# K-to-gate handover, blocked k, shared value buffers and branch A's split order in a one-core transformer block

## The chip, the cores and the metric

The kernel runs on one core of one Trainium2 chip. The metric is the device time of one execution in microseconds, the median over several runs. A profiled execution has a span, from its first to its last instruction, and a time of its own that is a little longer.

## The reference

One layer of a hybrid block over 1024 tokens of width 1024, in float32:

```python
h = rmsnorm(x, ln1_g[l]) * (1.0 + sc1) + sh1
p = h @ w_in[l]
q, k, v, cb, cc, cx, ga, gb = jnp.split(p, split_at, axis=-1)      # eight sections of 1024
q = rmsnorm(q.reshape(b, s_len, SB_HEADS, SB_HEAD_DIM), q_norm_g[l])   # 16 heads of 64
k = rmsnorm(k.reshape(b, s_len, SB_HEADS, SB_HEAD_DIM), k_norm_g[l])
...
y_a = stick_breaking_attention(q, k, v)
y_b = cb * causal_dwconv(cc * cx, conv_w[l])
merged = (jax.nn.sigmoid(ga) * (y_a @ w_branch_a[l])
          + jax.nn.sigmoid(gb) * (y_b @ w_branch_b[l]))
x = x + g1 * (merged @ w_out[l])
h = rmsnorm(x, ln2_g[l]) * (1.0 + sc2) + sh2
f = (jax.nn.silu(h @ w_ffn_gate[l]) * (h @ w_ffn_up[l])) @ w_ffn_down[l]
x = x + g2 * f
```

The modulations sh, sc and g come from a small product of the conditioning vector with `ada_w`.

## The kernel before

Every float32 product is computed from operands that are each split into a high part (ScalarE, a rounding copy) and a low part (VectorE, the difference), with three matmuls: high by high, high by low, low by high. Activations live on chip in four large tiles of 128 x 8 x 512: `hh[n]` is the high part and `hl[n]` the low part of the normalised input for token half n. Weights are loaded by SP's DMA queue into a small pool `raw` and split into the pools `whi` and `wlo`.

The program is one long sequence of stages, written in program order. A planner (a list scheduler that simulates times) fixes the order of instructions on each engine; each engine then runs strictly in that order and waits on semaphores. `tc.high_priority()` moves instructions ahead in the planner's order; `tc.issue_after(ins)` puts instructions of one engine behind `ins` on that engine. In some stretches `in_order` pins the order as written.

The stages are:

1. The start: the norm, the modulations, the splits of the input, half of v.
2. K (the loop over `cc` and `i`): for each half `cc` of the key width and each tile `i` of 128 tokens, `mm_tok` makes 24 matmuls into one PSUM bank. `finish_k` squares it (into a tile of the `wlo` pool, four slots), normalises it per head, transposes it on TensorE, splits it into `khl` and stores high and low part to DRAM (`d_k`) by ScalarE's DMA queue. The second halves of `finish_k` run one or two tokens later as `tails`. Beside K the generator `factors` prepares Strassen factors of the input in DRAM (`d_t`), which SP loads later.
3. The gates: 20 pairs of weight blocks (`gates`: q, the two convolution sections, the two gate sections), each computed with seven products in place of eight (Strassen's scheme in Winograd's form). Gate g needs two raw weights of 128 x 1024, the four quarters a11, a12 and a21, a22. GpSimd forms s3 = a11 − a21, s2 = a22 − s3, s1 = a21 + a22 and s4 = a12 − s2. The products are p1 (a11), p2 (a12), p6 (s2), p5 (s1), p7 (s3), p3 (s4) and p4 (a22), by the factors `fac[0]` to `fac[6]`. `first_two` makes p1 and p2 of gates 0 and 1 ahead of the stage, from raws that are loaded for that alone; gate 0 and gate 1 then load their two raws again. `fac[3]` lies over the first half of `hh[1]` and `hl[1]`, so it can be loaded only when K has read these. `fac[6]` (2 MB) and all of the stage's tiles lie in the pool `gp`, over the memory of K's weights and tiles. VectorE adds the products up; beside the last gates the later modulations are summed (`mods_later`, loads by ScalarE's queue). TensorE has six PSUM banks `pj` here.
4. The entry of attention: the second half of v is computed by `fillers`, first half e = 0 and then e = 1, each in eight blocks `i` of 24 matmuls of 256 columns. ScalarE evicts each block to a 256-wide tile `vs` (line 926) in the buffers of `ybh` and `ybl`, two of each, and SP stores it to `d_v`. The first half runs ahead of attention, beside the loads of heads 0 and 1 (`att_load`, with 64 partitions a load). Two PSUM banks `pj` serve here.
5. Attention over 16 heads, its TensorE order written out by hand, with the convolution branch and branch B's product as fillers between its steps.
6. Branch A: the attention output is read back from `d_ya` (`yr`), split into `ya` (line 1058 and the VectorE line behind it), and multiplied by `w_a` in 16 blocks; each is gated by sigmoid tiles and added to branch B's part. `preload_wo` loads five of the out projection's eight weight splits ahead (lines 1039 to 1044), through one raw slot.
7. The out projection, the second norm, the feed-forward part with Strassen again, and the output.

Line 132 to 134 are the three matmuls of a Strassen product, line 137 is the helper for two-operand element work on any engine, lines 309, 922 to 924 and 903 to 905 are the matmuls of K, of the value half and of the branches. Line 490 is the high half of `g_split`, line 412 the high half of k, line 479 a raw load, line 643 the load of `fac[6]`, line 554 the modulation sum, line 927 the store of a value block, line 1043 the high half of an out weight, line 1074 the gating of a block of branch A, line 1227 the first matmul of the out projection.

Of the kernel before, what the change touches and what calls it, by code (L numbers as in the profile page):

```python
# [30 lines left out]
def block_kernel(tc, x, x_t, cols, ada_1, ada_2, ada_row, w_q, w_kv, w_v1, w_cg, w_a, w_b, w_o, w_g, w_u, w_d, out):  # L31
# [36 lines left out]
    d_k = [drp.tile([KT, P, T], F32, name=f"d_k{e}") for e in range(2)]  # L68
# [327 lines left out]
    def finish_k(ps, i, ch):  # L396
# [54 lines left out]
    for cc in (1, 2):  # L451
        w = wq[4:] if cc == 1 else [load_w(w_kv[cc, j]) for j in range(4)]
        for i in range(8):
            ps = ps_pj()
            mm_tok(ps, i, w, 0, 8)
            while len(tails) >= 2:
                next(tails.pop(0), None)
            tails.append(finish_k(ps, i, cc - 1))
            next(tails[-1])
            for _ in range(2 if (cc, i) < (1, 4) else 3):  # L460
                more()
            if (cc, i) == (2, 1):
                for _ in ml:
                    pass
                s2b.close()
                sx.close()

    ftx = ExitStack()
    ftp = ftx.enter_context(tc.tile_pool(name="phft", bufs=1, side="right", reuse_waits="tile"))
    ft = {q: ftp.tile([P, 2, 4, 512], F32R, name=f"ft{q}") for q in (5, 4)}  # L470
    for q in (5, 4):
        nc.sync.dma_start(ft[q].bitcast(F32), d_t[q])

    def g_bank():
        return ps_pj()

# [16 lines left out]

    fac = {0: (hh[0][:, 0:4], hl[0][:, 0:4]), 1: (hh[0][:, 4:8], hl[0][:, 4:8]), 2: (hh[1][:, 4:8], hl[1][:, 4:8])}
    def g_prod(w, q):
# [4 lines left out]
    gates = ([(5, j) for j in range(4)] + [(sec, j) for j in range(4) for sec in (1, 2)] +  # L500
             [(sec, j) for sec in (4, 3) for j in range(4)])

    def w_of(sec, m):
        return w_q[m] if sec == 5 else w_cg[sec, m]

    pre = {}

    def first_two(g):
        sec, j = gates[g]
        raw = g_raw(w_of(sec, j))  # L510
        return g_prod(g_split(raw[:, :512]), 0), g_prod(g_split(raw[:, 512:]), 1)
# [7 lines left out]
    def two_raw(g):  # L519
        sec, j = gates[g]  # L520
        return g_raw(w_of(sec, j)), g_raw(w_of(sec, j + 4))
# [119 lines left out]
    raws = two_raw(0)  # L641
    pend, pmm, eq = [], [], end_q()
    nc.sync.dma_start(ft[6].bitcast(F32), d_t[6])
    for e in range(2):
        nc.sync.dma_start(fac[3][e].bitcast(F32), d_t[3][:, e])
    for g, (sec, j) in enumerate(gates):
# [38 lines left out]
        p6 = g_prod(g_split(s2_), 5)  # L685
# [934 lines left out]
```

## Time and profile before

| | |
|---|---|
| median of 3 runs | 1833.43 us (1831.43 to 1839.17) |
| profiled execution, own time | 1836.9 us |
| its span | 1835.0 us |
| TensorE busy | 1802.3 us (98%) |
| VectorE busy | 1353.1 us (74%) |
| ScalarE busy | 794.9 us (43%) |
| GpSimd busy | 366.7 us (20%) |
| mean granted TensorE clock | 0.996 |

A matmul of 512 columns shows as 0.39 us but the next one starts some 0.23 us later: they are pipelined, so the step between starts is the rate, and the time in brackets on a timeline row is real idle time. The granted clock is 1 nearly throughout; a window of few microseconds shows where it is not.

### The profile page before, as it was taken

The page shows a single profiled execution, that of the slowest core. Times are in us where ns is not written, and L with a number is a line of the kernel's source. Part 1 is how long each engine was busy: PE and PEld are TensorE (multiplying, and loading weights), DVE is VectorE, ACT ScalarE, POOL GpSimd, SP SyncE. Part 2 cuts the span into 40 slices and gives each one's busy share as a digit, 9 for nine tenths or more (in the row PEclk, how much of TensorE's full clock was granted, in tenths as well). Part 3 has the DMA queues.
Part 4 walks back from the last instruction along what each step waited for, and adds up shares of the span by engine and source line. Part 5 has one row for each costly group of instructions (what it writes and reads, how often), then busy time and mean ns, then how long its engine had stood idle before and what let it go on. Part 6 is the DMA issues. An engine that isn't in the chain of part 4 may idle for free.

```text
span 1835.0 us, 24920 instructions
## 1 busy us (share of the span) xinstructions
PE 1802.3 (98%) x8829; PEld 1503.8 (82%) x8829; DVE 1353.1 (74%) x1957; ACT 794.9 (43%) x1494; POOL 366.7 (20%) x277
## 2 busy tenths in 40 slices
PE   7999999999999999999999999999999999999999
PEld 4787778888878988888888788877888888888887
DVE  7874776779872789999888545589977788744776
ACT  3452553333332666666665311663444344422321
POOL 0043327423240000000000000105544454300000
PEclk9999999999999999999999999999999999999999
DMA  9598452227747467669654536424533344299766
GB/s 395 200 315 303 162 187 79 81 75 253 269 153 234 138 187 202 195 201 304 170 155 146 196 124 219 135 98 153 203 138 148 130 171 172 103 335 342 282 229 222
DMA packets 147268, 358.03 MB, mean 195 GB/s; under 512 B 15480, under 2 KB 44480, under 8 KB 144968
## 3 DMA queue, kind: packets, MB, share of 16 engines
q1 hardware_dynamic: 101816, 289.12, 46.6%
q10 hardware_dynamic: 44320, 63.64, 9.9%
q0 software_dynamic: 1008, 3.67, 0.5%
q8 instruction: 71, 1.16, 0.3%
q14 instruction: 53, 0.43, 0.1%
HBM read 245.74 MB, written 110.66 MB: 194 GB/s over the span
## 4 chain that ended last, share of the span: by engine, by line
PE 85%; DVE 6%; DMA 5%; issue 2%; ACT 1%; POOL 1%; SPq 0%; ACTq 0%; DVEq 0%; POOLq 0%
PE e L132 7%; PE e L134 7%; PE e L133 7%; PE pj L132 5%; PE pj L134 5%; PE pj L133 5%; PE pj L309 5%; PE pj L903 5%; PE pj L905 5%; PE pj L904 5%; PE e L1447 4%; PE e L1449 4%; PE e L1448 4%; PE tr L827 3%; PE o L843 2%; PE z L803 2%
## 5 line engine op out<-in xcount | busy, mean ns | idle before, releaser
L813 DVE TENSOR_TENSOR_SCAN pt<-pt,mk 128x128 f32<-128x128 f32 (+7 forms) x128 | 172.4, 1347 | 13.5 <-ACT pt L805 13.5
L132 PE MATMUL e<-big,whi 128*128 128x512 f32 x352 | 137.9, 392 | 2.0 <-DVE c L137 2.0
L134 PE MATMUL e<-big,wlo 128*128 128x512 f32 x352 | 137.7, 391 | 0.0
L133 PE MATMUL e<-big,whi 128*128 128x512 f32 x352 | 137.6, 391 | 0.0
L123 POOL TENSOR_SCALAR rs_m<-ss 128x1 f32<-128x1 f32 x8 | 2.1, 261 | 645.6 <-ACT xn L1250 645.6
L137 DVE TENSOR_TENSOR c<-e,c 128x512 f32<-128x512 f32 x138 | 92.8, 686 | 51.4 <-PE e L134 50.2
L132 PE MATMUL pj<-big,whi 128*128 128x512 f32 x320 | 125.2, 391 | 1.7 <-DVE c L137 1.7
L133 PE MATMUL pj<-big,whi 128*128 128x512 f32 x320 | 124.8, 390 | 0.0
L134 PE MATMUL pj<-big,wlo 128*128 128x512 f32 x320 | 124.4, 390 | 0.0
L1447 PE MATMUL e<-whi,f 128*128 128x512 f32 (+1 forms) x319 | 121.8, 382 | 0.6 <-ACT whi L1108 0.6
L137 DVE TENSOR_TENSOR wlo<-raw,whi 128x512 fp32r<-128x512 f32 x116 | 87.8, 761 | 46.9 <-ACT whi L490 46.2
L1448 PE MATMUL e<-wlo,f 128*128 128x512 f32 (+1 forms) x319 | 121.8, 382 | 0.0
L1449 PE MATMUL e<-whi,f 128*128 128x512 f32 (+1 forms) x319 | 121.7, 382 | 0.0
L831 DVE TENSOR_TENSOR atl<-tr,ath 128x512 fp32r<-128x512 f32 (+1 forms) x192 | 103.9, 551 | 19.1 <-ACT ath L830 17.6
L805 ACT ACTIVATE pt<-z,rq 128x512 f32<-128x512 f32 (+1 forms) x192 | 104.8, 575 | 27.2 <-PE z L804 27.1
L903 PE MATMUL pj<-big,whi 128*128 128x512 f32 x256 | 114.0, 445 | 0.0
L137 DVE TENSOR_TENSOR c<-pj,c 128x512 f32<-128x512 f32 x140 | 92.9, 681 | 28.0 <-PE pj L134 27.5
L137 POOL TENSOR_TENSOR ws<-raw,raw 128x512 f32<-128x512 f32 x40 | 56.7, 1417 | 282.0 <-DMA raw<-w_cg 161.3
L309 PE MATMUL pj<-whi,big 128*128 128x512 f32 x352 | 109.3, 396 | 3.6 <-ACT big L292 3.6
L490 ACT ACTIVATE whi<-raw 128x512 fp32r<-128x512 f32 x116 | 72.6, 629 | 82.7 <-PE pj L133 38.4
L830 ACT ACTIVATE ath<-tr 128x512 fp32r<-128x512 f32 (+1 forms) x192 | 93.2, 487 | 30.3 <-PE tr L827 29.4
L133 PE MATMUL e<-rl,whi 128*128 128x512 f32 x264 | 102.9, 390 | 1.5 <-DVE rl L137 1.5
(258 smaller groups left out, 5000.2 us busy)
## 6 DMA issues: line engine op xcount, KB each, us to landing
f<-d_f SPq DMA_DIRECT2D x77, 512.0 KB, 4.1
d_f<-fs SPq DMA_DIRECT2D x70, 512.0 KB, 3.2
raw<-w_cg SPq DMA_DIRECT2D x40, 512.0 KB, 4.7
raw<-w_u SPq DMA_DIRECT2D x26, 512.0 KB, 3.3
raw<-w_g SPq DMA_DIRECT2D x25, 512.0 KB, 3.4
ad<-ada ACTq DMA_DIRECT2D x19, 512.0 KB, 5.7
ada<-ada SPq DMA_DIRECT2D x8, 1024.0 KB, 13.5
d_t<-ts SPq DMA_DIRECT2D x16, 512.0 KB, 3.9
```

The source lines that it names most:

```text
L132: nc.tensor.matmul(ps, wh[:, k, :], fh[:, k, :], start=(k == 0), stop=False)
L133: nc.tensor.matmul(ps, wh[:, k, :], fl[:, k, :], start=False, stop=False)
L134: nc.tensor.matmul(ps, wl[:, k, :], fh[:, k, :], start=False, stop=(k == 3))
L137: eng.tensor_tensor(out=out, in0=a, in1=b, op=op)
L309: nc.tensor.matmul(ps, a, b, start=(k == 0 and q == 0), stop=(k == KT - 1 and q == 2))
L805: nc.scalar.activation(pt[:, off + s0:off + s0 + m], z[:, :m], AF.Sigmoid, scale=rq[:, 1, i, h:h + 1])
L813: nc.vector.tensor_tensor_scan(out=pt[:, rev], data0=pt[:, rev], data1=mk[:, rev], initial=1.0, op0=ALU.mult, op1=ALU.max)
L831: nc.vector.tensor_tensor(out=tl[:, :nb, c0:c0 + P], in0=src, in1=th[:, :nb, c0:c0 + P].bitcast(F32), op=ALU.subtract)
L903: nc.tensor.matmul(ps, wh, rh_, start=(k == 0), stop=False)
L1447: nc.tensor.matmul(o, sh, w[0][:, c], start=(j == 0), stop=False)
L1448: nc.tensor.matmul(o, sh, w[1][:, c], start=False, stop=False)
L1449: nc.tensor.matmul(o, sl, w[0][:, c], start=False, stop=(j == NJ - 1))
```

## The change

It has four parts, and no arithmetic changes.

- The handover from K to the gates. Only gate 1's early products have a raw of their own, which is loaded and split inside the K loop, ahead of token step 3 of the second half; gate 0's two raws are loaded there too, and its early products and its sums are made from the same two. In the second half of K the tokens run 4 to 7, then 0 to 3, and `fac[3]` is loaded at step 4. Gate 1's early products come first, then the tails, then gate 0's. The tiles of the sums have a pool of their own (`gp2`), and the pools' layout in memory is fixed by allocating the split tiles first. s3, s2 and the split of s2 (`w6`) are of high priority in gate 0; in all gates the split of s2 is written ahead of the next raws and of the copy of p1. `fac[6]` is loaded with high priority behind the last raw. In gate 0 the product p3 comes ahead of p7. The k tiles of the last two steps are stored by SP's queue, the others by ScalarE's as before.
- `d_k` is laid out in blocks of one token tile, so that a store writes rows of 2 KB in place of 512 bytes, and a load of a head's keys reads pieces of 512 bytes in place of rows of 4 KB.
- Two value evictions share a buffer of 512 columns, so that the four buffers hold eight.
- The loads and splits of `ya` are of high priority, and `preload_wo` is issued behind the last gating product written ahead of it (block 5, second half); this puts the VectorE instructions of `preload_wo` behind it.

```diff
-    d_k = [drp.tile([KT, P, T], F32, name=f"d_k{e}") for e in range(2)]
+    d_k = [drp.tile([2, KT, P, 4, P], F32, name=f"d_k{e}") for e in range(2)]
...
         for e, t in ((0, hi), (1, lo)):
-            nc.scalar.dma_start(d_k[e][4 * ch:4 * ch + 4, :, i * P:(i + 1) * P].rearrange("j p t -> p j t"),
-                                t.rearrange("p (j t) -> p j t", j=4).bitcast(F32))
+            q.dma_start(d_k[e][ch, i].rearrange("p j t -> p (j t)"), t.bitcast(F32))
...
+    def two_raw(g):
+        sec, j = gates[g]
+        return g_raw(w_of(sec, j)), g_raw(w_of(sec, j + 4))
+
+    for cc in (1, 2):
+        w = wq[4:] if cc == 1 else [load_w(w_kv[cc, j]) for j in range(4)]
+        for i_, i in enumerate(range(8) if cc == 1 else (4, 5, 6, 7, 0, 1, 2, 3)):
+            if (cc, i_) == (2,4):
+                for e in range(2):
+                    ld = nc.sync.dma_start((hh, hl)[e][1][:, 0:4].bitcast(F32), d_t[3][:, e])
+            if (cc, i_) == (2,3):
+                raw1 = g_raw(w_of(*gates[1]))
+                pre_w = [(g_split(raw1[:, :512]), g_split(raw1[:, 512:]))]
+                raws = two_raw(0)
+            ps = ps_pj()
+            mm_tok(ps, i, w, 0, 8)
...
+            tails.append(finish_k(ps, i, cc - 1, nc.sync if (cc, i_) > (2, 5) else nc.scalar))
...
-    for g in range(NG):
-        pre[g] = first_two(g)
-        if g == 0:
-            for tl in tails:
-                next(tl, None)
...
+    pre_w.append((g_split(raws[0][:, :512]), g_split(raws[0][:, 512:])))
+    pre = {1: tuple(g_prod(pre_w[0][q], q) for q in range(2))}
+    for tl in tails:
+        next(tl, None)
+    pre[0] = tuple(g_prod(pre_w[1][q], q) for q in range(2))
...
+    for t_ in ("whi", "wlo"):
+        gp.tile([P, 512], F32R, tag=t_, bufs=GS2, name=nm(t_))
     ft[6] = gp.tile([P, 2, 4, 512], F32R, name="ft6")
+    sg2 = ExitStack()
+    gp2 = sg2.enter_context(tc.tile_pool(name="phg2", bufs=1, reuse_waits="tile"))
...
-    raws = two_raw(0)
-    nc.sync.dma_start(ft[6].bitcast(F32), d_t[6])
-    for e in range(2):
-        nc.sync.dma_start(fac[3][e].bitcast(F32), d_t[3][:, e])
+    with tc.high_priority(), tc.issue_after(last_raw[0].ins):
+        nc.sync.dma_start(ft[6].bitcast(F32), d_t[6])
...
-        s1, s2_, s3, s4 = (gp.tile([P, 512], F32, tag=f"ws{q}", bufs=1, name=nm("ws")) for q in range(4))
-        tt(nc.gpsimd, s3, a11, a21, ALU.subtract)
-        tt(nc.gpsimd, s2_, a22, s3, ALU.subtract)
+        s1, s2_, s3, s4 = (gp2.tile([P, 512], F32, tag=f"ws{q}", bufs=1, name=nm("ws")) for q in range(4))
+        with tc.high_priority() if g == 0 else ExitStack():
+            tt(nc.gpsimd, s3, a11, a21, ALU.subtract)
+            tt(nc.gpsimd, s2_, a22, s3, ALU.subtract)
+            w6 = g_split(s2_)
...
-        p6 = g_prod(g_split(s2_), 5)
+        p6 = g_prod(w6, 5)
...
+        p3 = g_prod(g_split(s4), 2) if g == 0 else None
         p7 = g_prod(g_split(s3), 6)
...
-        p3 = g_prod(g_split(s4), 2)
+        p3 = p3 or g_prod(g_split(s4), 2)
...
-            nc.sync.dma_start(skh[es].bitcast(F32), d_k[0][pr, e0:e0 + DH, :])
+            nc.sync.dma_start(skh[es].rearrange("p (i t) -> p i t", t=P).bitcast(F32), d_k[0][pr // 4][:, e0:e0 + DH, pr % 4].rearrange("i p t -> p i t"))
...
-                vs = fq.tile([P, 256], F32, tag=("ybh", "ybl")[i % 2], bufs=2, name=nm("vs1"))
+                if i % 2 == 0:
+                    v2 = fq.tile([P, 512], F32, tag=("ybh", "ybl")[i // 2 % 2], bufs=2, name=nm("vs1"))
+                vs = v2[:, i % 2 * 256:i % 2 * 256 + 256]
...
+    with tc.high_priority():
+        for n in range(2):
+            for k in range(KT):
+                yr = fp.tile([P, 512], F32, tag="yr", bufs=2, name=nm("yr"))
...
         if (m, n) == (KT - 2, 0):
-            preload_wo()
+            with tc.issue_after(last_m.ins):
+                preload_wo()
...
-        nc.vector.tensor_tensor(out=sa, in0=ps, in1=sa, op=ALU.mult)
+        last_m = nc.vector.tensor_tensor(out=sa, in0=ps, in1=sa, op=ALU.mult)
```

More of the change, by code (lines that the diff above doesn't have):

```diff
@@ L449, in more @@
             next(ml, None)
[L451 to L475, printed above, removed]
     def g_raw(src):
@@ L492, in g_split, with w_of, g_bank @@
         return hi, lo
+    gates = ([(5, j) for j in range(4)] + [(sec, j) for j in range(4) for sec in (1, 2)] +
+             [(sec, j) for sec in (4, 3) for j in range(4)])
+    def w_of(sec, m):
+        return w_q[m] if sec == 5 else w_cg[sec, m]
+    def two_raw(g):
[13 more added lines that the diff above has]
+            mm_tok(ps, i, w, 0, 8)
+            while len(tails) >= 2:
+                next(tails.pop(0), None)
+            tails.append(finish_k(ps, i, cc - 1, nc.sync if (cc, i_) > (2, 5) else nc.scalar))
+            next(tails[-1])
+            for _ in range(2 if (cc, i_) < (1, 4) else 3):
+                more()
+            if (cc, i_) == (2, 1):
+                for _ in ml:
+                    pass
+                s2b.close()
+                sx.close()
+    ftx = ExitStack()
+    ftp = ftx.enter_context(tc.tile_pool(name="phft", bufs=1, side="right", reuse_waits="tile"))
+    ft = {q: ftp.tile([P, 2, 4, 512], F32R, name=f"ft{q}") for q in (5, 4)}
+    for q in (5, 4):
+        nc.sync.dma_start(ft[q].bitcast(F32), d_t[q])
+    def g_bank():
+        return ps_pj()
     fac = {0: (hh[0][:, 0:4], hl[0][:, 0:4]), 1: (hh[0][:, 4:8], hl[0][:, 4:8]), 2: (hh[1][:, 4:8], hl[1][:, 4:8])}
@@ L709, in block_kernel @@
             next(ml, None)
+    sg2.close()
     sg_.close()
```

33 lines of the change are left out of this document (9 added, 24 removed).

## The prediction

> **What bounds the kernel now.** I read the page first, then the waits of PE, then the timeline around each long wait. The page:
>
> ```profile
> span 1835.0 us, 24920 instructions
> PE 1802.3 (98%) x8829; PEld 1503.8 (82%) x8829; DVE 1353.1 (74%) x1957; ACT 794.9 (43%) x1494; POOL 366.7 (20%) x277
> PE 85%; DVE 6%; DMA 5%; issue 2%; ACT 1%; POOL 1%; SPq 0%; ACTq 0%; DVEq 0%; POOLq 0%
> ```
>
> TensorE is busy for 98% of the span and carries 85% of the chain that ended last. All idle time of PE is 1835.0 − 1802.3 = 32.7 us, so nothing that leaves its matmuls as they are can win more than that and what the clock adds. The diff adds and removes no matmul. The question is which idle stretches it ends. The view of PE's waits (who is waited for; us in total, times, longest) lists them:
>
> ```profile
> PE pj L922 <- ACT vs L926: 3.0, 1, 3.0
> PE pj L132 <- ACT whi L490: 2.7, 2, 2.3
> PE pj L903 <- ACT ya L1058: 1.3, 1, 1.3
> ```
>
> These three are where the diff works: the K-to-gate handover (2.26 of the 2.7), the value evictions (L926) and branch A's splits (L1058). The clock comes on top. Windows of equal length after the first two waits, beside an undisturbed one, and one that holds the third and what follows it (columns: window; its length, then busy time and instruction count of PE, weight loads, DVE, ACT, POOL; granted clock; DMA share; GB/s):
>
> ```profile
> 180.40:183.80 3.40, 3.40 (x10) 2.62 (x9) 2.99 (x5) 1.13 (x3) 0.03 (x1) 0.51 0.97 339
> 184.00:187.40 3.40, 3.40 (x16) 2.82 (x15) 0.01 (x1) 0.00 (x0) 0.20 (x1) 1.00 0.42 149
> 593.40:596.80 3.40, 3.19 (x15) 3.20 (x16) 0.00 (x0) 0.43 (x2) 0.00 (x0) 0.52 1.01 326
> 1017.00:1024.00 7.00, 5.65 (x25) 4.37 (x24) 5.64 (x9) 2.64 (x5) 0.00 (x0) 1.00 0.79 259
> ```
>
> After the first two waits the clock is near half for 3.4 us: 10 matmuls in place of 16. The third costs no clock. I price the clock at the part not granted: 3.4 x (1 − 0.51) = 1.7 and 3.4 x (1 − 0.52) = 1.6 us.
>
> **Part 1, the handover.** Timeline, PE first, then the other engines (start; us; engine line operation; in brackets the idle time before it and its releaser):
>
> ```profile
> 177.37 0.40 PE L134 MATMUL pj<-big,wlo 128*128 128x512 f32 x1
> 180.03 0.50 PE L132 MATMUL pj<-ft,whi 128*128 128x512 f32 x1 [2.26 <-ACT whi L490]
> 163.49 1.89 DVE L137 TENSOR_TENSOR wlo<-raw,whi 128x512 fp32r<-128x512 f32 x3
> 164.80 3.60 SPq L479 DMA_DIRECT2D raw<-w_q  x2
> 172.83 0.33 SPq L643 DMA_DIRECT2D ft<-d_t  x1
> 175.32 1.28 POOL L137 TENSOR_TENSOR ws<-raw,raw 128x512 f32<-128x512 f32 x1 [6.54 <-DMA raw<-w_q]
> 176.57 1.29 POOL L137 TENSOR_TENSOR ws<-raw 128x512 f32<-128x512 f32 x1
> 175.94 0.69 ACT L412 ACTIVATE khl<-tr,cst 128x512 fp32r<-128x512 f32 x1 [7.06 <-DMA d_k<-khl]
> 178.83 1.67 ACT L490 ACTIVATE whi<-ws 128x512 fp32r<-128x512 f32 x3
> ```
>
> The four products of gates 0 and 1 end at 177.8. The next one, p6, needs s2 = a22 − (a11 − a21) split in two. Both raw slots are held by the early products' weights until DVE writes their low halves (163.49), so gate 0's own two raws are issued only at 164.80 and after. They reach POOL at 175.32, s2 is ready at 177.86, and ACT, which had stood 7.06 us behind a store of k, splits it at 178.83. The new code loads only gate 1's first raw for the early products, splits it inside the K loop, and then loads gate 0's two raws, which serve both its products and its sums. s3, s2 and their split move ahead, with POOL idle (6.54 us before 175.32) and the sum tiles in a pool of their own. The tokens of the second K half run 4–7 first, so that hh[1]'s first half is free for its factor early. One 512 KB raw load goes. Every part of p6's chain has over 10 us then: gain 2.26 + 1.7 = 4.0 us.
>
> What is late next? p5's factor is loaded before the loop ends. p3 takes p7's place for gate 0, which gives factor 6 (2 MB, issued at 172.83 and in the new code after the last raw) one product more. Gate 1's sums come next: its raws wait for gate 0's slots. I count nothing for them because s2, s1 and s4 are made earlier too. If that cover is gone, the old wait of 2.26 us with its clock returns. In the K loop gate 1's two low halves hold two of the four slots that the squares also use. One token uses one slot at a time, so two are enough.
>
> The last two k tiles leave by SP's queue, behind raws and ahead of gate 1's raws: two issues a token, each about 0.33 us as the issue at 172.83, on a queue that waits for slots anyway. I price them at nothing.
>
> **Part 2, k in blocks.** Stores now write 2 KB rows, loads read 512-byte pieces in place of 4 KB rows. The DMA view (KB each; median us to landing) and two windows:
>
> ```profile
> d_k<-khl ACTq DMA_DIRECT2D x32, 256.0 KB, 6.1
> skh<-d_k SPq DMA_DIRECT2D x32, 256.0 KB, 4.5
> raw<-w_v SPq DMA_DIRECT2D x4, 512.0 KB, 5.1
> raw<-w_o SPq DMA_DIRECT2D x8, 512.0 KB, 7.0
> 584.00:590.00 6.00, 6.00 (x52) 6.00 (x52) 1.12 (x2) 1.27 (x3) 0.00 (x0) 1.00 1.04 219
> 599.00:600.00 1.00, 1.00 (x11) 1.00 (x10) 0.40 (x1) 0.91 (x2) 0.00 (x0) 1.00 0.99 294
> ```
>
> Stores: 6.1 us in 512-byte pieces, no PE wait rests on them beyond the 7.06 above, so nothing is counted. Loads: from 584 to 590 the queue holds key loads into 64 partitions, 4 KB a piece, and moves 219 GB/s at a full DMA. From 599 to 600 it holds value stores in 512-byte pieces and moves 294 GB/s. So short pieces do not bind sooner than the 64-partition loads already do. From these rows the extra is between 0 and, if the two limits added, 256 KB / 294 GB/s = 0.9 us a load. Only the eight loads of heads 0 and 1 stand in a full queue (0 to 7 us); later heads are loaded a head ahead, and 16 heads share the 415 us between 604.23 and 1019.12 below, 26 us each. I take 0, because the slower row is the one of the same loads.
>
> [...]
>
> **Part 3, value evictions.** PE, ACT and SP at the entry of attention:
>
> ```profile
> 593.61 0.58 PE L922 MATMUL pj<-whi,big 128*128 128x256 f32 x1 [3.02 <-ACT vs L926]
> 593.17 0.66 ACT L926 ACTIVATE vs<-pj 128x256 f32<-128x256 f32 x2 [5.34 <-DMA d_v<-vs]
> 584.04 5.04 SPq L927 DMA_DIRECT2D d_v<-vs  x4
> 589.97 1.57 SPq L479 DMA_DIRECT2D raw<-w_v  x2
> 598.94 2.07 ACT L490 ACTIVATE whi<-raw 128x512 fp32r<-128x512 f32 x3 [0.29 <-PE pj L924]
> 604.23 0.36 PE L922 MATMUL pj<-whi,big 128*128 128x256 f32 x1
> ```
>
> Four buffers take four evictions. The first store is issued at 584.04, behind the loads of heads 0 and 1, and the fifth eviction waits until 593.17 for it. Two PSUM banks are then full and PE stands 3.02 us. With two evictions to a 512-wide buffer all eight of the first half fit, and the second half finds its first buffer only after PE has gone through the remaining blocks. Gain 3.02 + 1.6 = 4.6. Next late: the second half's weights. Issued at 589.97 and, 5.1 us later by the row above, landed at 595.1; ACT splits them at 598.94 once PE frees the slots. 4.6 us earlier that is 594.3, so they are 0.8 us late, part of it hidden by the score matmuls ahead of 604.23. I take off 0.5. With the key loads at 0.9 us extra each instead, all 4.6 us would go.
>
> **Part 4, branch A and the out weights.**
>
> ```profile
> 1019.12 0.47 PE L903 MATMUL pj<-ya,whi 128*128 128x512 f32 x1 [1.35 <-ACT ya L1058]
> 1016.29 1.15 ACT L1043 ACTIVATE whi<-raw 128x512 fp32r<-128x512 f32 x2 [2.18 <-DMA raw<-w_o]
> 1017.35 0.61 ACT L1058 ACTIVATE ya<-yr 128x512 fp32r<-128x512 f32 x1
> 1079.29 0.69 DVE L1074 TENSOR_TENSOR sgi<-pj,sgi 128x512 f32<-128x512 f32 x1 [1.54 <-PE pj L905]
> 1100.85 0.39 PE L1227 MATMUL e<-whi,big 128*128 128x512 f32 x1
> ```
>
> The split of y that PE waits for stands on ACT behind a split of an out weight that itself waits for its load. Now y's splits are ahead and the out weights' low halves follow the product of block 5, which ends at 1079.29. Gain 1.35, no clock. The single raw slot then makes the out weights run in series: two loads at up to 7.0 us and ten ACT and DVE steps of about 0.65, some 20.5 us, within the 21.6 us up to 1100.85. Nothing is counted; without that cover up to 3 us.
>
> **Sum.** 4.0 + 4.6 + 1.35 − 0.5 = 9.5 us off the profiled execution's own 1836.9 us (span 1835.0): 1827.4. That execution is 3.5 us above the median of the three runs, 1833.43, so I put the same 9.5 us against the median: 1823.9, taken as 1824. About 0.5% (9.2 us) is what a measurement of this kernel can tell from no change, and the forecast stands just beyond it.
>
> [...]
>
> **The rivals.** *A fourth stall goes too.* In the gates:
>
> ```profile
> 508.58 2.02 POOL L137 TENSOR_TENSOR ws<-raw,raw 128x512 f32<-128x512 f32 x1 [25.81 <-DMA raw<-w_cg]
> 514.69 2.30 DVE L554 CUSTOM_DVE_ANT_0 uu<-uu,cab 128x1024 f32<-128x1024 f32 x1
> 517.65 0.50 PE L134 MATMUL pj<-ft,wlo 128*128 128x512 f32 x1 [2.10 <-DVE wlo L137]
> ```
>
> There a raw came late (POOL had idled 25.81 us), a modulation sum of 2.30 us took DVE ahead of a low half, and PE stood 2.10 us, with the half clock after it (1.7). The split of s2 is now written ahead of the next raws, the copies and these sums in every gate. If that ends this wait: 9.5 + 3.8 = 13.3, 1820. For it: DVE's order there is the planner's, which follows program order. Against: the raw's lateness is not touched.
>
> *The entry of attention stays full.* Key loads at the upper price eat part 3: 9.5 − 4.1 = 5.4, 1828. For: DMA is at 1.04 in the window. Against: the 219 GB/s.
>
> *The handover does not do what it says.* The planner places raws and sums where they were, because slots free as late: 9.5 − 4.0 = 5.5, 1828.
>
> *Slower.* The s2 split stands early in ACT's and DVE's order in all 20 gates. Where a raw is late, as at 508.58, ACT now waits on that split with the copy of p1 and the modulation loads behind it; PE then lacks a bank. The place is the eight gates of the two gate sections, the last of the 20, some 410 to 570 us, where these loads are issued. One such wait costs 2.1 + 1.7 = 3.8 us. To end 0.5% slower takes 9.5 + 9.2 = 18.7, five gates; at seven 26.6 − 9.5 = 17 us slower, 1850. Against: only one gate in eight is late now.
>
> **How the numbers follow.** Forecast (1821 to 1827) 0.52, of which 0.40 lies beyond 0.5%; fourth stall 0.17; entry full 0.09; no handover 0.07; slower 0.15. Faster 0.40 + 0.17 = 0.57; within 0.5%: 0.12 + 0.09 + 0.07 = 0.28; slower 0.15. The range reaches from the fourth stall with 2 us below it, 1818, to the two half gains with both together (−1.4 us), 1832; it leaves out the slower case.
>
> **What would show it.** In PE's waits the rows for L926 and the ya splits are gone, and no wait of over 2 us stands between K and the first gate; POOL's first sums start inside the K loop; the clock is whole there and after the first value half. Wrong would be: a PE wait for the second half's weights, for a key load, for an out weight near 1095, or several waits among those eight gates.

## The result, and the profile after

The changed kernel takes 1823.19 us (median of 5 runs, 1822.68 to 1827.39); the kernel before, timed beside it, 1836.92 (5 runs, 1831.43 to 1839.17). The ratio is 0.9936, 95% interval [0.9914, 0.9957]: some 12 us, or 0.6%, faster. Timed again on another chip ("after2" below) it was 0.9945 [0.9933, 0.9957], 10 us. The median of 1833.43 that the prediction started from lay low: beside the later kernels the kernel before has medians of 1836.1 to 1838.5.

The profiled execution took 1827.39 us, the slowest of the five, 9.5 us under the one of before. Its page:

```profile
span 1825.6 us, 24915 instructions
PE 1799.5 (99%) x8829; PEld 1502.2 (82%) x8829; DVE 1356.8 (74%) x1957; ACT 794.9 (44%) x1494; POOL 368.5 (20%) x277
```

PE is busy 2.8 us less than before, though it has the same matmuls; the mean granted clock is 0.997 where it was 0.996. Its idle time falls from 32.7 to 26.1 us. PE's waits (who is waited for; us in total, times, longest), those of over 1.2 us behind the start of the kernel:

```profile
PE pj L134 <- DVE wlo L137: 2.1, 1, 2.1
PE e L132 <- DVE c L137: 2.0, 1, 2.0
PE pj L908 <- DVE mb L982: 1.7, 1, 1.7
PE e L133 <- DVE rl L137: 1.5, 1, 1.5
PE pj L132 <- DVE c L137: 1.4, 1, 1.4
```

Two of the three waits that the prediction chose have gone without a successor: there is no row for a split of s2 (it was 2.3 on line 490, which is 463 now) and none for the value evictions (3.0 on line 926, now 933). The third has changed its name: 1.3 us on line 1058 became 1.7 us ahead of the same blocks (line 903 is 908 now), for an eviction on DVE. The wait of 2.1 us in the gates is as it was. The wait of 1.4 us there, for a sum at 446.72, is new; in the second trace of this kernel waits of 0.5 and 0.3 us stand in its place.

The handover in the timeline (start; us; engine line operation; in brackets the idle time before it and what ended it):

```profile
135.58 0.34 SPq L452 DMA_DIRECT2D raw<-w_q  x1
139.67 1.29 POOL L137 TENSOR_TENSOR ws<-raw,raw 128x512 f32<-128x512 f32 x1 [0.38 <-DMA raw<-w_q]
140.92 1.28 POOL L137 TENSOR_TENSOR ws<-raw 128x512 f32<-128x512 f32 x1
168.69 0.63 ACT L463 ACTIVATE whi<-ws 128x512 fp32r<-128x512 f32 x1 [1.87 <-PE pj L133]
172.73 3.65 SPq L415 DMA_DIRECT2D d_k<-khl  x4
```

s3 is formed at 139.67 where it was 175.32, and s2 right behind it. The split of s2 at 168.69 waits only for a slot. PE has no wait at all from 150 to 215 us. The windows where the clock was half before, and the entry of attention (window; length; busy time and count of PE, weight loads, DVE, ACT, POOL; granted clock; DMA share; GB/s):

```profile
173.00:176.40 3.40, 3.40 (x18) 2.81 (x17) 1.86 (x5) 2.09 (x4) 0.00 (x0) 1.00 0.57 220
176.40:179.80 3.40, 3.40 (x16) 2.82 (x15) 1.30 (x3) 1.13 (x3) 0.00 (x0) 1.00 0.96 296
586.00:592.00 6.00, 6.00 (x51) 5.91 (x50) 1.82 (x3) 2.73 (x6) 0.00 (x0) 1.00 0.96 336
```

All at full clock, and at the entry PE is busy for the whole 6 us while DMA moves 336 GB/s.

Where the time went along the kernel can be read from the starts of same-numbered matmuls of PE (numbers 1080, 2400, 2880, 5400 and 8760 of 8829). The figures are worked out from the traces: start in that trace less start in the profiled execution of before, in us.

| kernel | gates (before: 265.0) | past the gates (568.8) | attention (634.3) | past branch A's start (1061.0) | end (1818.8) |
|---|---|---|---|---|---|
| changed | −5.1 | −6.2 | −10.4 | −10.1 | −9.5 |
| changed, again | −4.6 | −7.6 | −11.7 | −11.3 | −12.0 |
| handover alone | −0.1 | −4.8 | −3.6 | −3.9 | −2.9 |
| k layout alone | +0.3 | −4.5 | −2.4 | −2.4 | −2.9 |
| handover and layout | −5.0 | −9.0 | −7.2 | −7.0 | −5.1 |
| handover, k's stores on SP | −4.4 | −6.7 | −6.7 | −6.7 | −6.0 |
| handover, layout and evictions | −4.4 | −9.3 | −12.5 | −12.3 | −12.8 |
| whole, old k layout | −2.4 | −6.4 | −9.1 | −9.2 | −9.9 |
| hold bound to ACT too | −4.6 | −8.5 | −12.3 | −14.0 | −14.4 |
| the same, again | −5.0 | −9.6 | −12.9 | −14.5 | −14.9 |
| the same, faster spread | −4.5 | −10.6 | −10.4 | −11.8 | −12.2 |
| evictions alone | +1.4 | −1.3 | −4.2 | −4.7 | −4.7 |
| branch A alone | +1.1 | −0.5 | +1.4 | +1.1 | +0.4 |

The kernel with the faster spread has another order of matmuls around 568.8, so its −10.6 there does not compare. The first column shows the handover, the step from the second to the third the entry of attention. The step from the first to the second column is no effect of the change that can be told apart: the layout alone "gains" 4.8 us there, the changed kernel 1.1. What differs there is the wait in the gates and the half clock behind it. They were largest in the profiled execution of before (2.1 us and a half clock, and 1.0 us shortly ahead of it); in the other traces the wait is 1.0 to 2.1 us.

### The profile page after: what moved, and what is told of

The parts are those of the page before. It is cut to its first block, busy times and chain, and to the rows that moved or that the text cites. A ratio compares the mean times of both kernels' runs of the same rounds, so it can differ in the third digit from the quotient of the medians.

```text
span 1825.6 us, 24915 instructions
## 1 busy us (share of the span) xinstructions
PE 1799.5 (99%) x8829; PEld 1502.2 (82%) x8829; DVE 1356.8 (74%) x1957; ACT 794.9 (44%) x1494; POOL 368.5 (20%) x277
## 4 chain that ended last, share of the span: by engine, by line
PE 86%; DVE 7%; DMA 4%; issue 1%; ACT 1%; POOL 0%; SPq 0%; ACTq 0%; DVEq 0%; POOLq 0%
PE e L133 7%; PE e L132 7%; PE e L134 7%; PE pj L134 5%; PE pj L132 5%; PE pj L133 5%; PE pj L309 5%; PE pj L908 5%; PE pj L910 4%; PE pj L909 4%; PE e L1456 4%; PE e L1458 4%; PE e L1457 4%; PE tr L832 3%; PE o L848 2%; PE z L808 2%
```

## The experiments

Each kernel is timed against the kernel before on the same chip; the ratio comes with its 95% interval.

**The handover alone** (the kernel before with the new K loop, early loads and sums; layout, evictions and branch A as before).

```diff
-            nc.scalar.dma_start(d_k[e][4 * ch:4 * ch + 4, :, i * P:(i + 1) * P].rearrange("j p t -> p j t"),
+            q.dma_start(d_k[e][4 * ch:4 * ch + 4, :, i * P:(i + 1) * P].rearrange("j p t -> p j t"),
...
+            if (cc, i_) == (2,3):
+                raw1 = g_raw(w_of(*gates[1]))
+                pre_w = [(g_split(raw1[:, :512]), g_split(raw1[:, 512:]))]
+                raws = two_raw(0)
```

> The kernel before with the handover alone (raws, token order, pools, early split of s2, p3 ahead of p7, last two k tiles by SP's queue); d_k, value buffers and branch A as before. Theory: the 2.26 us wait and its half clock go (-4.0 us), and the waits among the gates lose about 2 us as in the changed kernel: 5 to 7 us faster, no PE wait between K and the first gate. Rival: the wait also rested on k's stores in 512-byte pieces, behind which ACT stood 7.06 us; then a wait of 1 to 2 us stays there and the gain is 2 to 4 us.

Measured: 1833.19 us, ratio 0.9984 [0.9976, 0.9993], 3 us. The wait at the handover is gone, but the matmuls in the gates are where they were (−0.1): a new wait stands inside K. PE's waits, and ACT in the timeline:

```profile
PE tr L409 <- DVE qn L403: 2.6, 1, 2.6
```

```profile
143.12 14.88 ACTq L415 DMA_DIRECT2D d_k<-khl  x2
158.04 0.60 ACT L398 ACTIVATE qsq<-pj 128x512 f32<-128x512 f32 x1 [14.96 <-DMA d_k<-khl]
```

The first row merges the two stores of one k tile. In narrower windows each issue takes 0.37 us, and ACT stands between them:

```profile
143.12 0.37 ACTq L415 DMA_DIRECT2D d_k<-khl  x1
157.63 0.37 ACTq L415 DMA_DIRECT2D d_k<-khl  x1
```

What it stands for is an earlier store. The DMA view from 137.0 to 137.4, where the store issued at 137.19 lies (size; us to landing):

```profile
d_k<-khl ACTq DMA_DIRECT2D x1, 256.0 KB, 20.4
```

That store lands at 157.6, the second store is issued at 157.63, and the timeline names a landing of these stores as what ended ACT's 14.96 us. The square of the next tile stands behind this on ACT, with it the norm, and PE's transposes wait 2.6 us. A window behind that wait shows the clock at 0.58:

```profile
162.60:166.00 3.40, 3.40 (x12) 2.73 (x11) 2.02 (x5) 1.18 (x2) 1.83 (x2) 0.58 0.53 160
```

In the changed kernel, where the stores write 2 KB pieces, the store issued at 137.17 lands after 9.2 us, the two issues with the wait between them take 3.66 us, and the square waits for PE alone:

```profile
143.10 3.66 ACTq L415 DMA_DIRECT2D d_k<-khl  x2
147.84 0.60 ACT L398 ACTIVATE qsq<-pj 128x512 f32<-128x512 f32 x1 [4.76 <-PE pj L309]
```

**The k layout alone.**

```diff
-    d_k = [drp.tile([KT, P, T], F32, name=f"d_k{e}") for e in range(2)]
+    d_k = [drp.tile([2, KT, P, 4, P], F32, name=f"d_k{e}") for e in range(2)]
...
+            nc.scalar.dma_start(d_k[e][ch, i].rearrange("p j t -> p (j t)"), t.bitcast(F32))
```

> The kernel before with k in blocks of one token tile alone. Theory: no change within 1.5 us: key loads go on at 210 to 250 GB/s while the queue is full at the entry of attention, and k's stores land sooner than 6.1 us. Rival: 512-byte pieces cost up to 0.9 us a load, the eight loads of heads 0 and 1 hold the value stores behind them, and the wait for the eviction grows from 3.0 us to up to 9: 2 to 6 us slower.

Measured: 1835.89 us, 1.0003 [0.9993, 1.0013]. No change in the time. In this trace PE's wait for the value eviction is longer, as the rival says:

```profile
PE pj L921 <- ACT vs L925: 5.2, 1, 5.2
```

With the old layout and the old evictions it is 3.0, 3.1, 3.9 and 4.3 us in four kernels, with the new layout and the old evictions 3.6 and 5.2, so the traces do not tell a part of the layout in it from the scatter; the timing leaves it at most 2.4 us.

**Handover and layout together.** The edit is the two diffs above.

> The handover and the blocked k layout together, on the kernel before; the value evictions and branch A's part are left as before. Alone the handover brought 3 us and the layout nothing. Theory that the two need each other (in the handover's trace ACT stood 15 us for a k buffer whose stores in 512-byte pieces had not landed, and PE lost 2.74 us in K): with the layout ACT does not stand there, PE has no wait from 150 to 215, and the matmuls behind the handover are 5 to 6.5 us earlier than before; the whole 5 to 7 us less, ratio 0.9962 to 0.9973. Rival that the parts simply add: 3 us, 0.9984, with ACT's wait for k's stores still there.

Measured: 1831.79 us, 0.9970 [0.9960, 0.9980], 5.5 us. The gates are 5.0 us earlier and no wait is left in K. The point estimates (3 + 0 against 5.5) speak for the first theory; the intervals overlap. The traces speak for it more clearly: the earlier store lands after 9.2 us, and the row that took 14.88 us takes 3.62 now.

```profile
142.99 3.62 ACTq L415 DMA_DIRECT2D d_k<-khl  x2
```

The evictions are as before here, and the wait for them is longer than it was (3.0):

```profile
PE pj L927 <- ACT vs L931: 3.6, 1, 3.6
```

**Handover alone, k's stores moved to SP.** This takes the stores, and what they wait for, out of ACT's order.

```diff
-            tails.append(finish_k(ps, i, cc - 1, nc.sync if (cc, i_) > (2, 5) else nc.scalar))
+            tails.append(finish_k(ps, i, cc - 1, nc.sync if cc == 2 else nc.scalar))
```

> The handover alone with the old layout, as in the second run, with all of k's stores in the second stretch issued from SP's queue in place of ScalarE's (before: the last two tiles alone). It tells what it is that PE loses in K. Theory that the issue of the small pieces holds ScalarE's queue (14.88 us for two stores at 143 us, and the square of the next tile behind them): ScalarE is free, the wait of 2.6 us of PE at 159 is gone, and the time is that of handover and layout together, 5 to 6 us less than before, unless SP's loads for the gates come late by being held in its place. Rival that a buffer whose store has not landed is what is waited for: ScalarE still stands over 8 us, on the buffer and not on an issue, and the time stays at 0.998 to 0.9985.

Measured: 1831.00 us, 0.9963 [0.9951, 0.9976], as handover and layout together. SP's and ACT's timeline:

```profile
143.14 24.90 SPq L415 DMA_DIRECT2D d_k<-khl  x10
```

```profile
147.88 0.60 ACT L398 ACTIVATE qsq<-pj 128x512 f32<-128x512 f32 x1 [4.76 <-PE pj L309]
```

SP's row merges ten stores of five tiles, which PE makes some 5.9 us apart, so its 24.90 us are not time that SP is held. Nothing that PE needs stands behind them late, and ACT waits for PE alone. So what PE lost was ACT's standing in the middle of its stores, and no k buffer was lacking. This run does not tell a long issue from a wait for an earlier store. The trace of the handover alone does: the issues took 0.37 us each, and the wait was for a landing. Long issues do occur, on SP here up to 5.44 us (durations in ns, least, median, most):

```profile
L415 SPq DMA_DIRECT2D d_k<-khl x16: 359/378/5442, 137.2 to 175.8; - x16
```

**The whole change with the old layout.** All of the change but the layout diff above.

> The whole change with the old layout of k (stores of 512-byte pieces), everything else as changed. Theory that handover and layout need each other: the two stores issued from ScalarE's queue near 143 us hold that queue for 10 to 15 us again, where the whole change shows 3.66, PE waits 2 to 3 us in K near 159, and the time is 2 to 4 us over the whole change, ratio to before 0.9955 to 0.9970. Rival that the layout gives nothing in either kernel: as the whole change, 0.9936 to 0.9945.

In the timeline of ACT and PE, and a window behind the wait:

```profile
143.04 14.37 ACTq L415 DMA_DIRECT2D d_k<-khl  x2
...
161.65 0.63 PE L409 MATMUL tr<-dm,qn 128*128 128x128 f32 x4 [2.05 <-DVE qn L403]
```

```profile
162.00:166.00 4.00, 4.00 (x21) 3.32 (x20) 2.62 (x5) 1.18 (x2) 2.24 (x4) 1.00 0.62 188
```

Measured: 1827.01 us, 0.9948 [0.9935, 0.9962]. ACT's stand is back with 14.37 us (the earlier store lands after 19.9) and PE's wait with 2.05; this time the clock stays whole behind it. The gates are 2.4 us earlier, where the kernels with both parts have 4.4 to 5.1: the layout is worth 2.0 to 2.7 us of trace there. At the end of the trace it is −9.9, between the two traces of the changed kernel (−9.5 and −12.0), so neither that column nor the timing shows a gain for the whole. It came out at 0.9948, over the 0.9936 and 0.9945 of the whole change but inside their intervals, and under the range that I expected.

**The value evictions alone.**

```diff
-                vs = fq.tile([P, 256], F32, tag=("ybh", "ybl")[i % 2], bufs=2, name=nm("vs1"))
+                if i % 2 == 0:
+                    v2 = fq.tile([P, 512], F32, tag=("ybh", "ybl")[i // 2 % 2], bufs=2, name=nm("vs1"))
+                vs = v2[:, i % 2 * 256:i % 2 * 256 + 256]
```

> The kernel before with two value evictions to a buffer alone. Theory: the 3.02 us wait for the eviction and the half clock after it go: 4 to 5 us faster; the first score after the first value half at about 597.5 in place of 602.3. Rival: DMA is full from 580 to 600 us, so PE waits there for the second half's weights or a key load in its place: under 2 us faster.

Measured: 1832.52 us, 0.9983 [0.9974, 0.9991], 3 us. The wait for line 926 is gone. What else stands in PE's waits, the first row at the start of the gates, the other at the entry:

```profile
PE tr L600 <- ACT gt L592: 3.3, 2, 1.9
PE pj L923 <- DVE wlo L137: 0.3, 1, 0.3
```

The first row is a wait behind the old handover, 0.8 us in the trace of before and 3.3 here. It has nothing to do with the evictions (branch A's part alone has 3.0 us there) and hides part of their gain in this trace.

It also corrects the price of the handover. PE's gap ahead of p6 is 2.27 us here, but the half clock did not follow. Behind the gap PE is 1.5 us ahead of the trace of before; by 212 us it is 1.4 behind it (a window behind the gap, then GpSimd, VectorE and PE):

```profile
181.96:185.37 3.41, 3.41 (x17) 2.83 (x16) 1.17 (x2) 0.00 (x0) 0.00 (x0) 1.00 1.02 366
188.17 1.28 POOL L137 TENSOR_TENSOR ws<-raw,raw 128x512 f32<-128x512 f32 x1 [8.00 <-DMA raw<-w_q]
191.40 1.10 DVE L137 TENSOR_TENSOR wlo<-ws,whi 128x512 fp32r<-128x512 f32 x1 [4.82 <-ACT whi L490]
200.15 0.40 PE L600 MATMUL tr<-gt,sel 128*16 128x512 f32 x1 [1.42 <-ACT gt L592]
210.39 0.40 PE L600 MATMUL tr<-gt,sel 128*16 128x512 f32 x1 [1.87 <-ACT gt L592]
```

Gate 1's weights come late to GpSimd, VectorE stands 4.82 us for the split of their sum with gate 0's sums behind it, and PE waits at line 600 for what is made of these. In the trace of branch A's part alone, with a gap of 2.3 us ahead of p6, the waits at line 600 are 3.0 us, and PE is 1.1 us behind at 265. So what the half clock cost in the trace of before, 1.7 us by the prediction's estimate, was time for which PE would have waited a little later.

**Handover, layout and evictions** (all but branch A's part).

> As the run before this, with the wide value evictions as well, so the whole change but for branch A's part. Theory: the value evictions are worth 4 to 5 us on top, as in the trace of their run alone (2.9 us at the entry) and the stall that they remove (3.2 to 5.4 us with its slow clock): 9 to 12 us less than before, and within 1 us of the whole change, as branch A's part alone did nothing. Rival that branch A's part works only behind the others: 1.3 us or more slower than the whole change.

Measured: 1826.40 us, 0.9946 [0.9934, 0.9959], 10 us. On top of handover and layout the evictions bring 0.9970 − 0.9946, 4.4 us; in the traces the attention column goes from −7.2 to −12.5.

**The whole change, timed beside these.**

> The changed kernel as it is, timed beside the three that follow, so that they can be compared with it and not only with the kernel before. If the difference already measured holds: 0.9936 of before within 0.002, 9 to 14 us less. The trace should again have no PE wait between K and the gates, none at the entry of attention, the wait of about 2.1 us near 511, and 1.7 us ahead of the last blocks of branch A.

Measured: 1825.37 us, 0.9945 [0.9933, 0.9957]. Without branch A's part it was 0.9946: that part does nothing here either. The wait ahead of branch A's last blocks is 0.5 us in this trace and not the 1.7 expected, and a wait of 0.7 us stands in attention. The two traces of this one program differ by 2.5 us, and a part of it is the clock behind one wait. The matmul behind the wait, and windows of 3.41 us around it, first in the changed kernel's first trace:

```profile
511.45 0.50 PE L134 MATMUL pj<-ft,wlo 128*128 128x512 f32 x1 [2.09 <-DVE wlo L137]
508.79:512.20 3.41, 1.32 (x5) 0.80 (x6) 3.41 (x5) 2.12 (x5) 0.91 (x1) 1.00 0.51 160
512.21:515.62 3.41, 3.41 (x9) 2.65 (x8) 2.88 (x7) 2.69 (x5) 0.00 (x0) 0.50 0.78 259
```

and in this run:

```profile
511.62 0.50 PE L134 MATMUL pj<-ft,wlo 128*128 128x512 f32 x1 [2.09 <-DVE wlo L137]
507.14:510.55 3.41, 1.90 (x8) 0.93 (x6) 3.41 (x4) 2.44 (x5) 2.65 (x2) 1.00 0.09 33
510.56:513.97 3.41, 2.35 (x10) 1.98 (x11) 3.41 (x9) 1.08 (x3) 0.00 (x0) 1.00 0.76 262
513.97:517.38 3.41, 3.41 (x16) 2.82 (x16) 2.57 (x5) 2.08 (x4) 0.09 (x1) 1.00 0.79 276
```

The same gap of 2.09 us: half clock (0.50) and 9 matmuls behind it in the one, full clock (1.00) and 16 in the other. The windows are not chosen freely. In the traces of before and of the changed kernel's first run, the clock records up to the end of the program show half clock in pieces of 3.41 us, and the starts of these pieces lie whole multiples of 3.413 us apart: 99, 121 and 317 of them behind the first in before (180.49, then 518.41, 593.51 and 1262.52), 146 and 363 in the changed kernel (13.86, then 512.21 and 1252.90). With the spans of these two cut into stretches of that length, from 40 us on, PE was idle for 2.26, 2.10, 2.92 and 2.03 us in the stretches ahead of the four pieces of before and for 2.09 and 2.01 us ahead of the two of the changed kernel, and in no other stretch for more than 1.71 us. In the first trace above the gap lies whole in one window (PE busy 1.32 us, so 2.09 idle); in the second a boundary divides it, and no window has more than 1.51 us idle. That the place of a gap of some 2 us decides on the half clock fits these traces; no run was made to test it.

**Branch A's part alone** (the splits in `tc.high_priority()`, the out weights behind `last_m`).

```diff
+    with tc.high_priority():
...
+            with tc.issue_after(last_m.ins):
+                preload_wo()
```

> The kernel before with branch A's splits at high priority and the out weights behind the product of block 5 alone. Theory (from the changed kernel's trace): ACT still stands some 5.5 us behind the first out weight's split, and VectorE's eviction of branch B's last block now stands behind the late splits of y: a wait of about 1.7 us for the eviction in place of 1.35 us for the split, so no change within 1 us. Rival (the prediction's step): 1.35 us faster with no wait there.

Measured: 1835.86 us, 0.9998 [0.9989, 1.0008]. No change; in its own trace PE waits 1.0 us for the eviction, in place of 1.35 for the split. Why, the changed kernel's timeline shows, ACT first, then DVE and PE:

```profile
1000.60 1.15 ACT L1050 ACTIVATE whi<-raw 128x512 fp32r<-128x512 f32 x2 [5.51 <-DMA raw<-w_o]
1001.65 1.14 ACT L1066 ACTIVATE ya<-yr 128x512 fp32r<-128x512 f32 x2
1006.03 0.63 ACT L1066 ACTIVATE ya<-yr 128x512 fp32r<-128x512 f32 x1 [2.21 <-DMA yr<-d_ya]
1006.69 1.48 DVE L137 TENSOR_TENSOR ya<-yr,ya 128x512 fp32r<-128x512 f32 x2 [2.04 <-ACT ya L1066]
1008.21 0.69 DVE L982 TENSOR_TENSOR mb<-pj,sgi 128x512 f32<-128x512 f32 x1
1009.04 0.47 PE L908 MATMUL pj<-ya,whi 128*128 128x512 f32 x1 [1.71 <-DVE mb L982]
```

`last_m` is an instruction of VectorE, and the hold binds VectorE alone. On ACT the high halves of the first out weight still stand ahead of branch A's splits and wait 5.51 us for their load. The splits come late, their buffers free late, and so do the next loads of y. On DVE the raised priority puts y's low halves at 1006.69 ahead of an eviction of branch B, and PE waits for that bank.

**The hold bound to ACT too.**

```diff
-            with tc.issue_after(last_m.ins):
+            with tc.issue_after(last_m.ins), tc.issue_after(last_h.ins):
                 preload_wo()
...
-        nc.scalar.activation(mh[n][:, m, :], sa, AF.Copy)
+        last_h = nc.scalar.activation(mh[n][:, m, :], sa, AF.Copy)
```

> The whole change, and the hold on the out weights is made to bind ScalarE too: their splits are issued behind the last activation of the sixth pair of branch A's blocks, not only behind its last multiply on VectorE. Theory of the step that failed (ACT stands 5.5 us for the first out weight ahead of branch A's own splits, and an eviction on DVE waits behind those splits): ACT no longer stands there, the 1.71 us of PE before the last blocks of branch A shrink to under 0.4, and the kernel is 1.2 to 1.9 us faster than the whole change (0.9990 to 0.9993 of it) unless the out weights come late by as much. Rival that the loads of branch A's activations themselves land too late (their two buffers): the wait stays at 1.3 to 1.7 us and the time is the same within 0.5 us.

> The whole change with the hold on the out weights binding ScalarE too, once more: its first timing left it unclear against the whole change (0.9940 and 0.9945 of before). Theory from its trace (the wait ahead of branch A's last blocks, 0.5 to 1.7 us in the whole change, is none): 0.5 to 1.7 us faster than the whole change, 0.9930 to 0.9942 of before. Rival that the time comes back in the gates or the end: 0.9945 or more.

Measured: 1825.83 us, 0.9940 [0.9928, 0.9953], and 1823.00, 0.9924 [0.9911, 0.9936]. In both traces PE has no wait left between 960 and 1060 us, and from attention to past branch A's start 1.7 and 1.6 us are gained on the kernel before (−12.3 to −14.0, −12.9 to −14.5), where the changed kernel loses 0.3 and 0.4 in its two traces (in the second it gains 0.8 at branch A and loses more in attention). That the wait is gone is shown. That the kernel is faster than the changed one is likely (best of all kernels measured) but not settled: the intervals overlap.

**Modulation sums spread faster,** on top of the last kernel.

```diff
-        for _ in range((5 if sec in (3, 4) else 0) if g + 1 < len(gates) else 50):
+        for _ in range((6 if sec in (3, 4) else 0) if g + 1 < len(gates) else 50):
```

> As the run before, and the work for the modulation that is spread over the last gates goes at 6 steps a gate in place of 5, so that its last multiply-reduces on DVE (2.30 us) no longer lie in the last gate, where PE waits 1.3 to 2.1 us for a split (the fourth wait, which the change did not remove). Theory that those instructions in the last gate are the cause: that wait is under 0.5 us and the time 1 to 3 us less than the run before. Rival that DVE is simply full over the seven gates (14.00 of 14.00 us in four of the seven stretches of 14 us): the wait comes in an earlier gate, 1 to 3 us of it, and the time is the same within 0.5 us or longer.

Measured: 1824.68 us, 0.9930 [0.9918, 0.9943], no better than the kernel under it. Windows of 14 us in the last gates, of the kernel under it first:

```profile
490.00:504.00 14.00, 14.00 (x63) 11.61 (x62) 14.00 (x25) 3.02 (x5) 1.66 (x2) 1.00 0.85 275
504.00:518.00 14.00, 12.23 (x54) 9.78 (x54) 11.68 (x19) 6.90 (x12) 6.54 (x5) 1.00 0.52 183
```

and with the faster spread:

```profile
490.00:504.00 14.00, 12.71 (x57) 10.46 (x57) 12.25 (x23) 4.69 (x8) 1.31 (x2) 1.00 0.63 203
504.00:518.00 14.00, 14.00 (x63) 11.63 (x62) 8.09 (x12) 6.36 (x11) 5.55 (x5) 1.00 0.44 150
```

PE is whole from 504 to 518 now, where it stood 1.77 us before (1.07 in the second trace of that kernel), and stands 1.29 us from 490 to 504. DVE, the third figure behind the window's length, was full (14.00) ahead of the old wait. So the wait has moved a gate ahead, as the rival says. That VectorE's load alone makes it is not shown: ahead of the new wait too GpSimd had stood 17.39 us for a late weight, and a multiply-reduce of 2.31 us stands on VectorE shortly ahead of the split. What costs this kernel its time is not in the gates, where its matmuls at 533 us are 8.8 us earlier than before, against 8.5 and 9.6 in the two traces of the kernel under it. It is lost at the entry of attention, where PE now waits for the second half's value weights:

```profile
PE pj L927 <- ACT whi L463: 1.2, 1, 1.2
```

## Why the prediction was right

The time forecast (1824) was met, and its working held in the main at two of the four parts, with errors of both signs.

*Part 1, handover: right in mechanism, sized at −4.0, measured −4.4 to −5.1 with the new layout.* The 2.26 us went, and the half clock behind it was there in the profiled execution of before. But that its 1.7 us are a price of their own does not hold: in the evictions' own trace, with the old handover and the full clock behind its gap (1.00), PE was not earlier behind the first gates but 1.4 us later, for it waited at their sums. "I count nothing for them", said of gate 1's sums, left out this wait (0.8 us in the trace of before, 3.3 in that one, 3.0 in the trace of branch A's part alone); the new handover took it away too.

*Part 2, layout: 0 alone was right* (1.0003). The step that failed is "no PE wait rests on them beyond the 7.06 above, so nothing is counted", said of the stores of k: with the old stores the handover gives 0.1 and 2.4 us in two traces of the gates and 3 us by timing. The prediction saw ACT stand 7.06 us behind a store, but took it as harmless because no wait of PE rested on it in the old order. With the handover's loads in the same stretch a store took 20.4 us to land (14.1 in the trace of before), ACT stood for it between two later stores, and a wait of PE did rest on that. "I price them at nothing", said of the last two tiles' stores on SP, held: PE has no wait there.

On the loads the small pieces took some more DMA time, which the kernel's time does not show. From 560 to 1000 us the packets of the main DMA queue, in the handover alone and then in the layout alone (packets, MB, share of the 16 engines' time):

```profile
q1 hardware_dynamic: 37484, 82.52, 66.0%
q1 hardware_dynamic: 66050, 82.44, 68.6%
```

That is 0.80% for each MB with the old layout and 0.83% with the new one; before and the changed kernel have 0.78% (64.8% for 83.20 MB) and 0.81% (68.2% for 84.12 MB). From either pair I estimate 0.032% of the 440 us for each of some 83 MB, which makes 11.7 us in all and some 0.2 us more DMA time for each of the 64 loads of keys: nearer to the 0 that the prediction took than to its upper bound of 0.9.

*Part 3, evictions: −4.6 + 0.5 forecast; −4.2 in the changed kernel's trace, 4.4 by timing on top of handover and layout, 3 by timing alone.* The second half's weights are late by 0.3 us of PE in most traces with this part, against the 0.5 taken off. The wait that went was 3.0 us in the trace of before, but 3.1 to 5.2 in the five other kernels that have it still, so the stall is not one fixed size.

*Part 4, branch A: −1.35 forecast, nothing measured.* The step that failed is "Now y's splits are ahead". They are ahead on DVE only. With the order that this step assumed, made on purpose, 1.6 us of trace do come.

*Sum.* The trace gives −5.1 (handover with layout), −1.1 (gates), −4.2 (evictions), +0.3 (branch A), +0.6 (towards the end), −9.5 in all. That it equals the forecast 9.5 is a balance, and partly luck: the layout and the wait behind the old handover made up for branch A, and the profiled execution was the slowest of five. By timing the gain is 10 to 12 us, and the start from a median that lay low brought the time back to the forecast.

*Rivals.* The fourth stall did not go by the change: 2.1 us at 511 in both traces. The reason given against it holds there: the weight is as late as before (GpSimd stood 23.59 and 24.49 us for it, 25.81 before), and a modulation sum of 2.30 us still stands ahead of the low half. The entry did not stay full and the handover did not stay where it was. In the gates one wait of 1.4 us came in the changed kernel's first trace and none of this size in the second, so ACT and DVE were not blocked there as the slower rival says.

*The clock.* Behind the stalls that went, the half clock that was priced at 1.7 and 1.6 us was there in the profiled execution of before (0.51 and 0.52 in windows of 3.4 us). As prices of a gap these terms were too firm. Gaps of 2.26 us (before, clock 0.51 in the window behind it) and 2.58 us (handover alone, 0.58) brought the half clock, gaps of 2.27 us (evictions alone, 1.00) and 2.05 us (whole change with the old layout, 1.00) did not, and 2.09 us brought it in one execution (0.50) and not in another of the same program (1.00): no fixed charge for a gap fits these runs. What fits the traces of before and of the changed kernel is the idle time within one stretch of 3.413 us, 2.01 us or more ahead of each half clock and at most 1.71 us elsewhere.

## What to carry to other kernels

When loads are moved into a stretch, look for stores issued by a compute engine there, and ask what they wait for and what is queued behind them: in the handover alone two issues of 0.37 us each, with a wait for an earlier store between them, kept ACT's next square back by 14.96 us. A merged row hides whether the time is an issue or a wait; narrow the window. Cut a change into parts and also run them in pairs: a part that did nothing alone (the layout, 1.0003) set free the gain of another (0.9984 to 0.9970). Before a half clock behind a wait is counted as a price of its own, look whether PE waits again a little later, as it did here for 3.3 us with the evictions alone (0.8 in the trace of before). When an order is to be forced, check each engine on its own: the hold on an instruction of VectorE left ACT standing 5.51 us for an out weight.

## What the runs showed of the hardware

- A store of k of 256 KB issued near 137 us took 14.1, 20.4 and 19.9 us to land in 512-byte pieces (before, handover alone, whole change with the old layout) and 9.2 us in 2 KB pieces (changed kernel, handover and layout). Single issues of these stores took up to 3.42 us on ACT (before) and 5.44 us on SP (k's stores moved to SP) in 512-byte pieces, up to 0.57 us (changed kernel) and 0.78 us (layout alone) in 2 KB pieces.
- A PE gap of 2.09 us was followed by half clock (0.50) in the changed kernel's first trace and by full clock (1.00) in its second. In the traces of before and of the changed kernel's first run, from 40 us on, the half clock came in six pieces of 3.41 us, in each trace whole multiples of 3.413 us apart. In the stretch of that length ahead of each, PE was idle for 2.01 to 2.92 us, and in no other for more than 1.71 us.
- Loads of k in 512-byte pieces into 64 partitions took, by estimate from the queue's shares (0.80 and 0.83% for each MB), some 0.2 us more of DMA time a load than in 4 KB rows, and cost nothing that can be measured in the kernel's time (layout alone, 1.0003 [0.9993, 1.0013]).
